# Hybrid block on one core: six tiles of the second attention allocated first, and the state-space constants recorded inside the first attention's weight units

## The chip, the cores and the metric

The kernel runs on one core of a Trainium2 chip. The metric is the device time of one execution in microseconds, as the median of several runs. The profile is of one execution.

## What is computed

The reference is one encoder block on 1024 tokens of width 1024. RMS norm; then two branches: a state-space branch and a forgetting attention of 8 heads of 128, merged by sigmoid gates; then a second norm and a retrieval of 16 of 16,384 experts for each of 8 heads (PEER). The part that the change touches:

```
step = exp(log_step)[:, None]
mag = exp(ar * step)
lam_re = mag * cos(ai * step);  lam_im = mag * sin(ai * step)
...
br = coef_re[..., None] * b_re - coef_im[..., None] * b_im
bi = coef_re[..., None] * b_im + coef_im[..., None] * b_re
...                                    # scan with lam over the tokens
s = einsum('bhqd,bhkd->bhqk', q_blk, k) * scale + c_blk[..., None] - cum
p = softmax(where(key_pos <= q_pos, s, -inf));  o = p @ v
```

## The kernel before

The tokens are worked in two groups of 512. `front(g)` is a generator for one group, and the main order (L1218 to L1240) resumes the two generators in turn. For group 0 it runs: the norm with its transposes to `hT`, a stop; the forget logits (the pool `fg`: `lg`, `cum`, `rows`), the first projections (the pool `upr`: two units of part "first", their results `ut` stored to `d_u`), then the attention (pool `att0`), the state-space scan, the gated merge, and the query of the expert search. For group 1 the scan stands before the attention `att1`. After both, `dense()` does the expert matmuls (L1135, L1195), the longest part of the time.

A weight matrix comes in units. `unit()` (L431) loads two halves of one (`wraw`, L446, on SP's queue), ScalarE makes the rounded half of `ws` (L447), VectorE (DVE) the remainder (L448), and for group 0 SP stores the split weights (`d_w`, L450) for group 1 to read back. `ws` has four buffers, so two units are in flight, and `wraw` two. An attention pass goes over four head pairs `hp`; each has the units query, key, value and gate. TensorE (PE) multiplies them at L460 (by token) and, for the gate, at L466. Then for each of the two heads: transposes of queries and keys (L640), scores (L682, L684, L686), softmax on DVE and ScalarE (L689 maximum, L692 exponential, L694, L695), transposes of the probabilities (L707, copied out at L711 and L712), product with the values (L715, L717).

`s5_setup()` (L184) is a second generator that makes the state-space constants. Up to its first `yield` it issues seven loads (L188), then one long chain of DVE instructions, most of 128x16 elements, and near the end six of 128x2304 (L340 to L345) and six of 128x2048 that leave `win` (L358 to L363). After that it stops after every small piece: eight of transposes of `win` on PE (L369, copied by ScalarE at L372, stored to `d_sw`), eight of matmuls `kz` (L387). `unit()` of part "att" in group 0 resumes it SETUP = 2 times before its own loads, and the remainder is drained at the last head pair.

What sets the order: the program is recorded as Python runs, and a scheduler then puts each engine's instructions in one fixed row, by a time line it keeps and by the order of recording. On the chip each engine takes its row in order. SP issues most DMAs and waits in its row for what they need. Tiles of a pool get addresses in the order in which they are first asked for; a tile on memory that an earlier one held waits for that one's last use. `att1` lies on the memory of the query phase of group 0: `h2T` at the bottom, above it `tops` (lists of the top search) and `sk`, `q`, `sc`, `wf`.

The main order before, of which the change drops the second resumption:

```
    first, second = front(0), front(1)
    setup = s5_setup()
    next(first)
    next(setup)
    next(first)
    next(second)
```

Of the kernel before, what the change touches and what calls it, by code (L numbers as in the profile page):

```python
# [20 lines left out]
FT = mybir.dt.float32  # L21
FR = mybir.dt.float32r
# [10 lines left out]
P = 128  # L33
# [24 lines left out]
def kernel(ctx: ExitStack, tc: tile.TileContext, x, w_in, w_f, w_query, w_out, w_glu,  # L58
# [351 lines left out]
    def pump(n, m=0):  # L410

        for i, (work, k) in enumerate(((pending, n), (gating, m))):
            left[i] += k
            while left[i] >= 1 and work:
                left[i] -= 1
                if next(work[0], True):
                    work.pop(0)
            if not work:
                left[i] = 0.0


    def front(g):
        t0, GT = GROUPS[g]
        NB, NC, B0 = GT // P, GT // L, t0 // P
# [68 lines left out]
        with tc.tile_pool(name=f"fg{g}", bufs=1, side="left", reuse_waits="tile") as sp:  # L493
# [6 lines left out]
            n = 0  # L500
# [107 lines left out]
        ap_ctx = ExitStack()  # L608
        sp = ap_ctx.enter_context(tc.tile_pool(name=f"att{g}", bufs=1, side="left", reuse_waits="tile"))
        pj = apart[0] if g else sp  # L610
        for hp in range(4):
            if g == 0 and hp == SCAN:
                for _ in setup:
# [45 lines left out]
            for h in range(2):  # L659
# [5 lines left out]
                nc.gpsimd.dma_start(rq, d_cq[hd, :, t0:t0 + GT])  # L665
                keys = [(kT[:, h], t0)]
                if g:
                    kp = sp.tile([P, 2, t0], FR, name="kp")
                    nc.gpsimd.dma_start(kp, d_k[hd][:, :, :t0])
                    vp = sp.tile([P, B0, 2, P], FR, name="vp")  # L670
                    nc.gpsimd.dma_start(vp, d_v[hd][:, :B0])
                    keys.insert(0, (kp, 0))
                probs = []
                for b in range(NB):
                    ps = psum.tile([P, S], FT, name="S", bufs=2)
                    qs = slice(b * P, (b + 1) * P)
                    for kt, k0 in keys:
                        last = k0 == t0
                        n = (b + 1) * P if last else t0
                        o = ps[:, k0:k0 + n]  # L680
                        for z, (i, j) in enumerate(PASSES):
                            nc.tensor.matmul(o, qT[:, h, i, qs], kt[:, j, :n], start=(z == 0), stop=False)  # L682
                        if last:
                            nc.tensor.matmul(o[:, n - P:n], idb, later, start=False, stop=False,  # L684
                                             skip_group_check=True)
                        nc.tensor.matmul(o, rq[:, qs], rk[:, k0:k0 + n], start=False, stop=True)  # L686
                    n = t0 + (b + 1) * P
                    nm = sp.tile([P, 1], FT, name="nm", bufs=4)
                    nc.vector.tensor_reduce(nm, ps[:, :n], axis=AX, op=OP.max, negate=True)  # L689
                    pr = sp.tile([P, n], FT, name=f"pr{b}")  # L690
                    sm = sp.tile([P, 1], FT, name="sm", bufs=4)
                    nc.scalar.activation(pr, ps[:, :n], AF.Exp, bias=nm, accum_out=sm)  # L692
                    ri = sp.tile([P, 1], FT, name="ri", bufs=4)
                    nc.vector.reciprocal(ri, sm)  # L694
                    nc.vector.tensor_scalar(pr, pr, ri, 2.0, op0=OP.mult, op1=OP.mult)  # L695
                    probs.append(pr)
                    pump(*BESIDE["score"])
# [27 lines left out]
        sp = ap_ctx.enter_context(tc.tile_pool(name=f"ssm{g}", bufs=1, side="left", reuse_waits="tile"))  # L725
# [84 lines left out]
        with tc.tile_pool(name=f"mix{g}", bufs=1, side="left", reuse_waits="tile") as sp:  # L810
# [35 lines left out]
            sp = nx.enter_context(tc.tile_pool(name=f"query{g}", bufs=1, side="left", reuse_waits="tile"))  # L846
# [369 lines left out]
    wp_ctx = ExitStack()  # L1216
    wp = wp_ctx.enter_context(tc.tile_pool(name="wraw", bufs=1, side="right"))
    first, second = front(0), front(1)  # L1218
    setup = s5_setup()
    next(first)  # L1220
    next(setup)
    next(first)
    next(second)
    next(second)
# [80 lines left out]
```

## Time and profile before

| | |
|---|---|
| median of 3 runs | 3405.45 us (3402.02 to 3405.73) |
| the profiled execution | 3406.96 us, span 3405.2 us |
| mean granted TensorE clock | 0.967 of full |
| PE busy | 3223.5 us, 95% of the span |
| DVE busy | 2596.6 us, 76% |
| ScalarE busy | 1222.5 us, 36% |
| GpSimd (POOL) busy | 1030.5 us, 30% |
| chain that ended last | PE 79%, DVE 8%, DMA 7% |

Busy time of an engine is the time in which it had an instruction in work. "PE idle" is the time between two of its matmuls. In a row of a timeline, the bracket at the end gives the idle time of the engine just before the row, and after the arrow the instruction whose end let it go on.

### The profile page before, as it was taken

To read this page: it belongs to the slowest core of one execution; us is meant where nothing else is said; L and a number is where in the kernel's file an instruction comes from. 1 tells how busy PE (TensorE), PEld (TensorE's weight loads), DVE (VectorE), ACT (ScalarE), POOL (GpSimd) and SP (SyncE) were. 2 spreads that over 40 slices of the span, in tenths; PEclk is the share of its full clock that TensorE was granted. 3 is DMA by queue.
4 is the path that set the end of the run, shared out by engine and by line. 5 is a ranking of instruction groups with operands and counts; after the bars stand their busy time and mean duration, and the time that the engine had idled before them with its cause. 6 is when DMAs were issued, how large, how long until landed. Compare 5 with 4: busy or idle time off the path is not lost.

```text
span 3405.2 us, 52100 instructions
## 1 busy us (share of the span) xinstructions
PE 3223.5 (95%) x18959; PEld 2870.8 (84%) x18959; DVE 2596.6 (76%) x5493; ACT 1222.5 (36%) x2693; POOL 1030.5 (30%) x831
## 2 busy tenths in 40 slices
PE   7899888979999797899999999999999999999998
PEld 6788677868788686789999998989889898888887
DVE  7645554688776677669898788889897888888886
ACT  4444232323455355414774222222222222222221
POOL 0000000002222021200213464555465555554553
PEclk9899798989999898899999999999999999999999
DMA  7877786757576599965979798989899899988996
GB/s 255 286 269 276 251 322 249 264 202 258 177 229 220 175 315 305 326 228 172 255 217 320 273 363 287 353 306 351 301 360 339 315 339 333 346 314 299 347 332 212
DMA packets 465315, 965.44 MB, mean 284 GB/s; under 512 B 198304, under 2 KB 226208, under 8 KB 440480
## 3 DMA queue, kind: packets, MB, share of 16 engines
q1 hardware_dynamic: 345872, 545.43, 46.9%
q0 software_dynamic: 119184, 416.67, 34.4%
q8 instruction: 149, 2.44, 0.3%
q14 instruction: 110, 0.90, 0.1%
HBM read 775.84 MB, written 186.12 MB: 283 GB/s over the span
## 4 chain that ended last, share of the span: by engine, by line
PE 79%; DVE 8%; DMA 7%; issue 3%; ACT 2%; SPq 1%; POOL 1%; DVEq 0%; ACTq 0%; POOLq 0%
PE mm L1135 25%; PE S L1195 18%; PE mm L460 10%; PE mm L466 8%; PE tp L1195 5%; PE tp L1083 4%; PE S L715 2%; PE S L682 2%; PE S L466 2%; DMA vraw<-in_uv_dram 1%; PE S L686 1%; DMA wraw<-in_w_in_dram 1%; PE tp L707 1%; DVE r L990 1%; DMA r<-in_uv_dram,idx 1%
## 5 line engine op out<-in xcount | busy, mean ns | idle before, releaser
L1135 PE MATMUL mm<-dhT,us 128*128 128x320 f32 x6144 | 973.9, 310 | 3.0 <-ACT us L1127 1.6
L1135 PEld LDWEIGHTS mm<-dhT,us 128*128 128x128 f32 x6144 | 929.1, 188 | 29.3 <-ACT us L1127 2.2
L1195 PE MATMUL S<-vs,w 128*128 128x512 f32 x3072 | 794.9, 393 | 3.6 <-ACT vs L1192 3.3
L982 POOL DMA_INDIRECT r<-in_uv_dram,idx x384 | 476.0, 1240 | 833.3 <-DVE dots L990 494.3
L982 POOL DMA_INDIRECT r<-in_uv_dram,second x384 | 518.8, 1351 | 584.4 <-DVE acc L988 419.6
L1195 PEld LDWEIGHTS S<-vs,w 128*128 128x128 f32 x3072 | 566.9, 189 | 111.1 <-ACT vs L1192 4.8
L460 PE MATMUL mm<-ws,hT 128*128 128x256 f32 x3456 | 457.1, 290 | 49.3 <-ACT qkraw L625 26.2
L988 DVE SCALAR_TENSOR_TENSOR acc<-r,dots,acc 128x1024 f32<-128x1024 f32 x384 | 491.2, 1279 | 11.0 <-DMA r<-in_uv_dram,second 8.9
L460 PEld LDWEIGHTS mm<-ws,hT 128*128 128x128 f32 x3456 | 435.5, 196 | 61.2 <-ACT qkraw L625 29.2
L990 DVE CUSTOM_DVE_ANT_0 r<-r,h 128x1024 f32<-128x1024 f32 x384 | 465.4, 1219 | 27.7 <-DMA r<-in_uv_dram,idx 27.6
L1192 ACT ACTIVATE vs<-vraw 128x512 fp32r<-128x512 f32 x256 | 160.2, 628 | 385.4 <-DMA vraw<-in_uv_dram 213.4
L1195 PE MATMUL tp<-vs,w 128*128 128x512 f32 x768 | 259.2, 392 | 2.9 <-ACT vs L1192 2.9
L1127 ACT ACTIVATE us<-uraw 128x512 fp32r<-128x512 f32 x256 | 160.1, 627 | 258.2 <-PE mm L1135 236.3
L1128 DVE TENSOR_TENSOR us<-uraw,us 128x512 fp32r<-128x512 f32 x256 | 175.0, 685 | 97.2 <-ACT us L1127 94.8
L1137 ACT ACTIVATE ag<-mm 128x320 f32<-128x320 f32 x256 | 111.3, 435 | 361.1 <-PE mm L1135 333.5
L1193 DVE TENSOR_TENSOR vs<-vraw,vs 128x512 fp32r<-128x512 f32 x256 | 174.6, 686 | 73.4 <-ACT vs L1192 71.5
L663 POOL DMA_DIRECT2D rk<-d_ck x16 | 9.3, 580 | 722.6 <-DVE t L586 372.6
L1069 ACT ACTIVATE two<-two,eT 128x128 f32<-128x128 f32 x640 | 202.5, 391 | 55.2 <-DVE two L1066 48.9
L466 PE MATMUL mm<-h2T,ws 128*128 128x512 f32 x768 | 185.0, 398 | 0.0
L1083 PE MATMUL tp<-one,two 128*128 128x128 f32 x1280 | 175.6, 284 | 8.2 <-ACT sg L1084 3.9
L1083 PEld LDWEIGHTS tp<-one,two 128*128 128x128 f32 x1280 | 165.7, 196 | 15.7 <-ACT two L1069 5.2
L1195 PEld LDWEIGHTS tp<-vs,w 128*128 128x128 f32 x768 | 143.9, 188 | 33.4 <-ACT vs L1192 3.4
(310 smaller groups left out, 3758.0 us busy)
## 6 DMA issues: line engine op xcount, KB each, us to landing
d_w<-ws SPq DMA_DIRECT2D x76, 1024.0 KB
ws<-d_w SPq DMA_DIRECT2D x76, 1024.0 KB
uraw<-in_ut_dram SPq DMA_DIRECT2D x256, 256.0 KB
vraw<-in_uv_dram SPq DMA_DIRECT2D x256, 256.0 KB
gs<-d_g SPq DMA_DIRECT2D x32, 1280.0 KB
d_g<-sg SPq DMA_DIRECT2D x40, 960.0 KB
wraw<-in_w_in_dram SPq DMA_DIRECT2D x44, 512.0 KB
d_a<-ag SPq DMA_DIRECT2D x32, 320.0 KB
```

Of the source, the lines that this page charges most:

```text
L460: nc.tensor.matmul(o, act[:, k, i, b * P:(b + 1) * P], w[k // 4][:, k % 4, j, :], start=(n == 0), stop=(n == 23))
L466: nc.tensor.matmul(o, w[k // 4][:, k % 4, i, c * P:(c + 1) * P], act[:, k, j, :], start=(n == 0), stop=(n == 3 * kk - 1))
L982: nc.gpsimd.indirect_dma_start(out=r, out_offset=None, in_=halves, in_offset=bass.IndirectOffsetOnAxis(ap=at, axis=0))
L988: nc.vector.scalar_tensor_tensor(acc, r, dots[:, k:k + 1], acc, op0=OP.mult, op1=OP.add)
L990: nc.vector.tensor_tensor_reduce(r, r, h2, 1.0, 0.0, op0=OP.mult, op1=OP.add, accum_out=dots[:, k:k + 1])
L1069: nc.scalar.activation(two[:, t, :], two[:, t, :], AF.Copy, scale=eT[:, 2, t1 + t:t1 + t + 1])
L1083: nc.tensor.matmul(pg[:, t, :], two[:, t, :], one[:, t, :], start=True, stop=True)
L1128: nc.vector.tensor_sub(us[:, :, 1, :], raw, us[:, :, 0, :])
L1135: nc.tensor.matmul(pa, parts[k // 4][:, k % 4, i, :], hT[:, k, j, ts], start=(n == 0), stop=(n == 23))
L1192: nc.scalar.activation(vs[:, 0, :], raw, AF.Copy)
L1193: nc.vector.tensor_sub(vs[:, 1, :], raw, vs[:, 0, :])
L1195: nc.tensor.matmul(out_of[b], w[:, p, b * P:(b + 1) * P], vs[:, q, :], start=(i == 0 and p == q), stop=(i == C8 - 1 and q == 1))
```

## The change

It does two things. In the second attention (g = 1) the six tiles `pr0` to `pr3`, `kp` and `vp` are allocated at the start of the pool; where they were allocated before, they are now taken from a dictionary. They get the bottom of the pool, on `h2T`; the tiles that lay there (`qT`, `kT`, `vs`, then `rk`, `rq`) move up, onto `tops`, `sk`, `q`, `sc` and `wf`. And the main order no longer resumes `setup` between the norm and the forget logits, so that the first resumption is that of the first "att" unit of group 0, the query unit of the first head pair. All instructions are the same in number on each engine.

```
         pj = apart[0] if g else sp
+        sooner = {}
+        if g:
+            sooner.update({f"pr{b}": sp.tile([P, t0 + (b + 1) * P], FT, name=f"pr{b}") for b in range(NB)})
+            sooner["kp"] = sp.tile([P, 2, t0], FR, name="kp")
+            sooner["vp"] = sp.tile([P, B0, 2, P], FR, name="vp")
+
+        def of_pool(name, shape, dtype):
+            return sooner.pop(name) if name in sooner else sp.tile(shape, dtype, name=name)
...
-                    kp = sp.tile([P, 2, t0], FR, name="kp")
+                    kp = of_pool("kp", [P, 2, t0], FR)
...
-                    vp = sp.tile([P, B0, 2, P], FR, name="vp")
+                    vp = of_pool("vp", [P, B0, 2, P], FR)
...
-                    pr = sp.tile([P, n], FT, name=f"pr{b}")
+                    pr = of_pool(f"pr{b}", [P, n], FT)
...
     next(first)
-    next(setup)
     next(first)
```

The order on DVE at the start, before: the end of the norm of group 0 (`hT`), split weights `ws`, then the state-space constants from `er` on (`lp` and `kz` are their tiles too).

```order
L448 TENSOR_TENSOR ws<-wraw,ws 128x4x256
L174 TENSOR_TENSOR hT<-tp,hT 128x4x128 x3
L275 MEMSET lp 128x16
L276 MEMSET lp 128x16
L390 MEMSET kz 128x4x128 x2
L448 TENSOR_TENSOR ws<-wraw,ws 128x4x256
L174 TENSOR_TENSOR hT<-tp,hT 128x4x128
L206 TENSOR_SCALAR er<-ls 128x16
L206 TENSOR_SCALAR en<-er 128x16
```

And with the change; `rows` is the end of the forget logits, and the four `ws` in one row are the query's and the key's weights of the first head pair, the two behind them the value's.

```order
L520 TENSOR_SCALAR rows<-rows 8x512
L521 TENSOR_SCALAR rows<-rows 8x512
L448 TENSOR_TENSOR ws<-wraw,ws 128x4x256 x4
L275 MEMSET lp 128x16
L276 MEMSET lp 128x16
L390 MEMSET kz 128x4x128 x2
L448 TENSOR_TENSOR ws<-wraw,ws 128x4x256
L206 TENSOR_SCALAR er<-ls 128x16
L206 TENSOR_SCALAR en<-er 128x16
L204 TENSOR_SCALAR en<-en 128x16
L448 TENSOR_TENSOR ws<-wraw,ws 128x4x256
```

The constants moved from behind the norm to behind the forget logits and the weights of the query, the key and half of the value. The seven loads L188 moved alike on SP's row: from before the store of the second unit's last split weights to behind the store of the key unit's.

The order on PE in the first head pair, before: the last scores of the first head, then the first `kz` matmuls, and matmuls of the next unit (L460) around the transposes of the probabilities (L707; the four tiles of probabilities have numbers).

```order
L682 MATMUL S<-kT,qT 128x512 x3
L684 LDWEIGHTS idb
L684 MATMUL S<-later,idb 128x128
L686 MATMUL S<-rk,rq 128x512
L387 MATMUL mm<-co,win 128x128 x8
L460 MATMUL mm<-ws,hT 128x256 x24
L707 MATMUL tp<-idf,pr_1401 128x128
L707 MATMUL tp<-idf,pr_1415 128x128
L707 MATMUL tp<-idf,pr_1429 128x128
L707 MATMUL tp<-idf,pr_1443 128x128
L460 MATMUL mm<-ws,hT 128x256 x23
L715 MATMUL S<-pT,vs 128x512 x2
```

And with the change, whose lines are eleven higher here (L693 is L682 of before, L718 is L707, L726 is L715).

```order
L693 MATMUL S<-kT,qT 128x512 x3
L695 LDWEIGHTS idb
L695 MATMUL S<-later,idb 128x128
L697 MATMUL S<-rk,rq 128x512
L369 MATMUL tp<-idf,win 128x128 x4
L718 MATMUL tp<-idf,pr_1393 128x128
L718 MATMUL tp<-idf,pr_1407 128x128
L718 MATMUL tp<-idf,pr_1421 128x128
L718 MATMUL tp<-idf,pr_1407 128x128
L718 MATMUL tp<-idf,pr_1421 128x128
L718 MATMUL tp<-idf,pr_1435 128x128 x2
L726 MATMUL S<-pT,vs 128x512 x2
```

The `kz` matmuls and the next unit's matmuls moved behind both heads of the first pair, where 96 of L460 stand in one row. Up to the first L369 both orders have the same matmuls.

## Rows read from the trace of the kernel before

**Rows 1.** The page's busy time, share of the span and instructions of each engine.

```profile
PE 3223.5 (95%) x18959; PEld 2870.8 (84%) x18959; DVE 2596.6 (76%) x5493; ACT 1222.5 (36%) x2693; POOL 1030.5 (30%) x831
```

**Rows 2.** Stretches: length; busy of PE, PEld, DVE, ACT, POOL; clock, DMA share, GB/s.

```profile
28.00:109.60 81.60, 77.59 (x556) 71.20 (x555) 70.48 (x234) 29.44 (x70) 1.25 (x2) 0.97 0.82 275
...
114.30:185.60 71.30, 65.73 (x441) 58.11 (x442) 33.10 (x67) 33.55 (x92) 2.59 (x4) 0.88 0.72 266
...
1160.00:1440.00 280.00, 232.04 (x1422) 209.05 (x1421) 208.16 (x385) 139.54 (x359) 60.79 (x53) 0.88 0.98 313
```

**Rows 3.** PE's timeline: start, duration, line, operation, count, idle before and releaser.

```profile
93.78 3.53 PE L460 MATMUL mm<-ws,hT 128*128 128x256 f32 x25
...
114.24 0.88 PE L369 MATMUL tp<-idf,win 128*128 128x128 f32 x6 [4.28 <-DVE win L363]
...
119.61 1.12 PE L640 MATMUL tp<-idf,qkraw 128*128 128x128 f32 x4 [2.16 <-ACT wt L372]
...
137.74 3.15 PE L460 MATMUL mm<-ws,hT 128*128 128x256 f32 x24 [0.69 <-ACT kz L391]
...
183.07 2.65 PE L460 MATMUL mm<-ws,hT 128*128 128x256 f32 x20 [0.40 <-DVE vs L653]
185.56 1.04 PE L640 MATMUL tp<-idf,qkraw 128*128 128x128 f32 x8
```

**Rows 4.** DVE's timeline in the same columns, from the constants' first row to their last.

```profile
32.92 0.18 DVE L206 TENSOR_SCALAR er<-ls 128x16 f32<-128x16 f32 x1 [1.09 <-DMA ls<-in_log_step_dram]
...
52.65 0.17 DVE L282 TENSOR_TENSOR t<-lp 128x16 f32<-128x16 f32 x1
...
76.18 1.23 DVE L448 TENSOR_TENSOR ws<-wraw,ws 128x1024 fp32r<-128x1024 f32 x1 [2.75 <-ACT ws L447]
...
111.90 2.29 DVE L363 TENSOR_TENSOR win<-win,tc 128x2048 f32<-128x2048 f32 x1
```

**Rows 5.** ScalarE's timeline at the end of the first pair's query unit.

```profile
73.94 0.38 ACT L625 ACTIVATE qkraw<-mm 128x256 f32<-128x256 f32 x1 [1.63 <-PE mm L460]
...
75.10 1.05 ACT L447 ACTIVATE ws<-wraw 128x1024 fp32r<-128x1024 f32 x1
```

**Rows 6.** SP's timeline of DMA issues: the log steps, and the key unit's second store.

```profile
29.41 0.43 SPq L188 DMA_DIRECT2D ls<-in_log_step_dram  x1
...
65.67 0.63 SPq L450 DMA_DIRECT2D d_w<-ws  x1
```

**Rows 7.** Groups by line, DVE, 52.6 to 114.25: count, busy, mean ns, idle before.

```profile
L448 DVE TENSOR_TENSOR ws<-wraw,ws 128x1024 fp32r<-128x1024 f32 x7 | 8.5, 1221 | 5.0 <-ACT ws L447 5.0
L635 DVE TENSOR_TENSOR qkraw<-qkraw,rs 128x1024 f32<-128x1024 f32 x2 | 2.4, 1220 | 0.0
L653 DVE TENSOR_TENSOR vs<-mm,vs 128x256 fp32r<-128x256 f32 x4 | 1.7, 421 | 0.2
```

**Rows 8.** DVE's timeline in the first head: maximum, last probabilities, copy of the transposed.

```profile
135.12 0.67 DVE L689 TENSOR_REDUCE nm<-S 128x1 f32<-128x512 f32 x1
...
136.84 0.49 DVE L695 TENSOR_SCALAR pr<-pr,ri 128x512 f32<-128x512 f32 x1
...
141.99 0.69 DVE L712 TENSOR_TENSOR pT<-tp,pT 128x512 fp32r<-128x512 f32 x1 [4.67 <-ACT pT L711]
```

**Rows 9.** PE's waits, 1140 to 1440: line, what for, us in total, times, longest.

```profile
PE mm L466 <- ACT tg L792: 6.9, 3, 5.1
...
PE mm L460 <- DVE tg L803: 3.6, 1, 3.6
```

**Rows 10.** PE's timeline at the start of the second attention.

```profile
755.14 31.28 PE L460 MATMUL mm<-ws,hT 128*128 128x256 f32 x240 [23.80 <-ACT qkraw L625]
...
797.39 1.07 PE L682 MATMUL S<-kp,qT 128*128 128x512 f32 x4
```

**Rows 11.** POOL's timeline at the same place.

```profile
746.31 0.75 POOL L669 DMA_DIRECT2D kp<-d_k  x1 [21.02 <-DVE tops L161]
...
785.75 1.88 POOL L982 DMA_INDIRECT r<-in_uv_dram,idx  x1 [35.37 <-DMA top<-d_s]
```

## Prediction

> **What bounds the kernel now.** I read the page's busy shares first, then a table of busy times by stretch, then TensorE's own timeline in the stretch the change touches, and last the other engines' rows that TensorE waits for there. TensorE (PE) is busy 95% of the span [rows 1], so a delay that makes PE idle is not made up later unless some later idle time of PE shrinks for a reason of its own. The stretch table [rows 2] shows where there is such idle time: 81.6 - 77.6 = 4.0 us in the first projections (28 to 109.6), 71.3 - 65.7 = 5.6 us at 114.3 to 185.6, and 280 - 232 = 48 us at 1160 to 1440.
>
> The wait that matters is the 4.28 us before 114.24 [rows 3]: PE has done the first head pair's gate matmuls and stands at the transposes of `win` (L369), the last of the state-space constants, which VectorE (DVE) writes at L363. So the constants are already the last thing to arrive there: they begin on DVE at 32.92, end at 111.90 + 2.29 = 114.2 [rows 4], and PE is only 4.3 us ahead of them. There is no slack under which a later start of this chain could hide.
>
> **The change, part by part.** (1) *The constants.* Dropping the second statement of the main order takes the seven loads and the whole chain up to `win` out of the time before the forget logits and puts them into the first "att" unit. The generator stops for the first time only behind L363, so all 194 DVE instructions still come in one piece. Nothing is added or removed; what changes is each engine's row order. On DVE the chain's first row (L206) now stands behind nine rows of the first projections and behind the split of the value unit's first weights (L448). That split ran at 76.18 in the trace, after 2.75 us of waiting for ScalarE's half of it [rows 4], which started at 75.10 [rows 5]. In the changed order ScalarE's half waits only for the end of the query unit's matmuls, which the timeline puts a little earlier (ScalarE drew the last of them at 73.94), so I take 74 to 76 us for the chain's start instead of 32.9. The loads stand on SP's queue behind the second store of the key unit's split weights, which was issued at 65.67; seven issues of 0.43 us and some 3.5 us to land (the log steps went out at 29.41 and were used at 32.92 [rows 4, 6]) end by about 73, so they are not what is late.
>
> How far does DVE get? In the old order the first part of the chain runs from 32.92 to 52.65 [rows 4], 19.7 us with the forget logits and two weight splits among it. In the new order three splits (1.22 us each), the normalisation of queries and keys and two value splits (0.42 each) stand among it instead [rows 7], about as much, so I take 20 us again, and DVE reaches the split of the next pair's first weights at about 96. That row waits for a weight buffer which the value unit's matmuls release; their last row ends at 93.78 + 3.53 = 97.3 [rows 3], plus 1.05 us of ScalarE [rows 5]: about 98.5. From there the rest of the chain remains. It took 114.2 - 52.6 = 61.6 us, in which the rows of others took 8.5 (L448 x7), 2.4 (L635 x2), 1.7 (L653 x4) and some 1.9 (eleven small normalisation rows), and the wait before the splits 5.0 [rows 7]: 61.6 - 14.5 - 5.0 = 42 us of its own, a small wait or two in it. With four weight splits and a value row between (4 x 1.22 + 0.42 = 5.3) that is 46 to 48 us: `win` is ready at 98.5 + 48 = 146.5, rounded to 147 (between 143, if the first part is quick and the small gaps close, and 151, if weight loads that now go before the stores are late). Against 114.2 this is **+33 us** (29 to 37). PE reaches the wait at 109.6 as before or two or three microseconds sooner, and idles about 37 us instead of 4.3. What PE saved by then is worth nothing, since `win` sets the end of the wait.
>
> Why can't PE do something else? PE takes its rows in order, and both orders have the same rows up to L369 (480 of L460 with the logits among them, 48 of L466). Everything of the first pair's heads stands behind it.
>
> (2) *The first two heads.* Behind `win` there is the same PE work up to the L640 at 185.56: some 430 instructions, 65.7 us busy in 71.3 [rows 2, 3]. But its order differs. Before, next unit's matmuls (L460 x24 at 137.74 and others) run while the softmax of a head is made; now both heads stand there alone and the L460 come behind them. A head's own chain is then open: from the last scores to the last probabilities 135.12 to 137.33 = 2.2 us, the copies of their transposes 0.69 on DVE [rows 8] and about as much on ScalarE ahead of it, with the hand-overs about 4 us a head, 8 in all; before, PE lost 2.2 us there in five waits, of which 0.69 at 137.74 is the longest and 0.40 at 183.07 the last [rows 3]. The first L640 moves ahead of four transposes and saves up to the 2.16 us wait at 119.61 [rows 3]. Net 8 - 2.2 - 2 = **+4 us** (0 to +10).
>
> The clock there: PE's granted clock is 0.88 of full in 114.3 to 185.6, against 0.97 before it [rows 2]; four transposes of L640 took 1.12 us at 119.61, eight took 1.04 at 185.56 [rows 3], so PE starts this stretch at its lower level (1.2 GHz) after its idle time. I have counted the start at the rows' own slow pace. By the Trainium skill (TensorE: Matmul & The Clock Gate, Part 1: The HAM clock gate) the lower level is the default and activity releases it; by that, sparse heads after 37 idle us would stay at 1.2 GHz longer than the trace shows, which is the first rival below.
>
> (3) *Later.* From about 240 us on PE's rows stand in the same order, and so does nearly everything up to the gated merge of group 0. A store and two chunk loads (`uc`) now stand behind a store of the second pair on SP: 0 to +5 us, I take 0. In 1160 to 1440 the scheduler has interleaved the merge's loads and fill matmuls differently. PE's own waits for the merge's tiles there are 6.9 us (L466 on ScalarE's tg) and 3.6 us (L460 on DVE's tg) [rows 9], beside others; I take 0, with -10 to +10. From the dense experts on the orders are alike.
>
> (4) *The second attention's pool.* `pr0` to `pr3`, `kp` and `vp` move to the bottom, onto group 0's query input, and `qT`, `kT`, `vs`, `rk`, `rq` move up onto the lists of the top search. In the trace `kp` waits 21.02 us for the lists and is issued at 746.31 [rows 11], yet its first matmul is at 797.39 [rows 10]; that is 51 us of cover. PE's 23.80 us wait that ends at 755.14 is for ScalarE's `qkraw` [rows 10], whose tile lies in another pool. Pool engine's next row, a gather, waits for the top lists themselves until 785.75 whenever `kp` goes [rows 11]. Of the tiles moved up, `qT` and `kT` are written just ahead of those scores and `vs` one unit earlier, so the lists, done by 746, have been stored long before. So **0** (-2 to +2: a slip of the first `rk`, which the scores at 800 need, or a few DVE rows put otherwise).
>
> **Sum.** 33 + 4 + 0 + 0 + 0 = +37 us. The profiled execution took 3406.96 (span 3405.2), 1.5 above the median 3405.45; 3406.96 + 37 = 3444, less 1.5: **3443 us** as a median.
>
> **Rivals.** *Clock and open heads cost more.* If PE stays at 1.2 GHz through both heads, their some 20 us of high-pace work (ten a head, by what the second head took before) grows by 8 to 15 us where it is not hidden by waits. For it: rows of 114 to 134 are at that level after only 4.28 us idle. Against: 24 matmuls of L460 took 3.15 us at 137.74, 20 took 2.65 at 183.07 [rows 3], so PE was at the higher level (2.4 GHz) again by the first. 3443 + 12 = 3455.
>
> *The merge gives it back.* One mechanism on the other side: in 1160 to 1440 PE idles 48 us [rows 2], since gate matmuls and the next norm wait for merge tiles; the new order holds blocks of up to 18 gate matmuls between expert transposes, which could fill those holes. At 12 us regained the time is 3431; it must regain over 30 us (within 0.2%, 3412) or 44 us (faster, under 3399) to decide, more than four fifths of all idle time there. Against: the waits named sum to about 20 us and the same loads still have to land on a DMA that is busy 0.98 of that stretch [rows 2].
>
> *The change doesn't delay the chain.* If DVE reached the chain early enough to have `win` by 109.6, the time would be 3405 - 4 = 3401. It would have to start about as early as before; DVE's rows in order exclude this unless the value unit's weights came 40 us sooner.
>
> **How the numbers follow.** Forecast (+22 to +48, centre 3443) 0.75; clock and open heads (3453 to 3462) 0.10; merge gives back 8 to 20 us (3423 to 3435) 0.06; merge gives back most, or the chain isn't late: 0.04 within and 0.05 under. 0.2% (6.8 us) is about what a measurement of this kernel can tell from no change: within is 3398.6 to 3412.3. So faster 0.05, same 0.04, slower 0.91. The range 3424 to 3460 leaves out the last two cases, the best of the third and the ends of the second.
>
> **What would show it.** In the profile after: L206's first row at 74 to 76; L363 ending near 147; one PE wait on DVE `win` of 35 to 39 us in place of 4.28; no L460 between the L682 of the first two heads; the L640 of 185.56 near 222; the second attention's 23.8 us wait as it is. A `win` wait under 20 us would prove the DVE count wrong; a full wait with a smaller total would put the gain in 1160 to 1440.

## The result, and the profile after

The changed kernel takes **3436.89 us** (median; 3430.64 to 3443.29), the kernel before 3405.59 beside it (3398.73 to 3408.57): a ratio of 1.0096, 95% interval 1.008 to 1.0112, that is 27 to 38 us more (the two medians alone differ by 31.3). Forecast were 3443 us, in a range of 3424 to 3460.

The profiled execution after has a span of 3428.9 us and is the shortest that was timed; against the 3405.2 of before the spans differ by 23.7 only. The page's busy line answers to [rows 1]; columns as there.

```profile
PE 3218.2 (94%) x18959; PEld 2867.4 (84%) x18959; DVE 2597.7 (76%) x5493; ACT 1226.5 (36%) x2693; POOL 1034.3 (30%) x831
```

The number of instructions is the same on each engine, so nothing was added. PE is idle for 3428.9 - 3218.2 = 210.7 us, against 3405.2 - 3223.5 = 181.7: **29 us more idle time**, and 5.3 us less busy time. Most of the latter lies in the last 48 us of both traces, in which the same kind of row was slower in the profiled execution of before, at a granted clock of 0.90 against 0.98; I put it down to that execution and not to the change. Groups by line, PE, of these 48 us (instructions, busy time and mean ns of one), of before and then of after:

```profile
L1195 PE MATMUL S<-vs,w 128*128 128x512 f32 x124 | 33.4, 412 | 0.0
```

```profile
L1206 PE MATMUL S<-vs,w 128*128 128x512 f32 x136 | 34.1, 389 | 0.0
```

With both groups of that line there PE got through 156 rows before and 172 after.

Where the idle time lies is seen in PE's timeline after (columns as in [rows 3], to which these rows answer).

```profile
94.37 11.07 PE L466 MATMUL mm<-hT,ws 128*128 128x512 f32 x48
...
139.11 0.69 PE L369 MATMUL tp<-idf,win 128*128 128x128 f32 x2 [33.68 <-DVE win L360]
...
143.77 2.70 PE L369 MATMUL tp<-idf,win 128*128 128x128 f32 x10 [3.97 <-DVE win L363]
...
148.10 1.12 PE L651 MATMUL tp<-idf,qkraw 128*128 128x128 f32 x4 [0.78 <-ACT wt L372]
...
180.85 11.75 PE L460 MATMUL mm<-ws,hT 128*128 128x256 f32 x96
...
217.32 1.03 PE L651 MATMUL tp<-idf,qkraw 128*128 128x128 f32 x8
...
792.82 1.44 PE L460 MATMUL mm<-ws,hT 128*128 128x256 f32 x5 [23.32 <-ACT qkraw L636]
```

PE is through with the first pair's gate matmuls at 105.4 and then stands for 33.68 + 3.97 = 37.65 us at the transposes of `win`, where it stood for 4.28 before; `win` has two halves, from L360 and L363, and each is waited for. The whole delay is in one place. The next table compares the times at which the two traces reach the same matmul (L651 after is L640 of before):

```
place                                      before    after     after - before
last half of win arrives (L369)            114.24    143.77    +29.5
next pair's first transposes (L640 x8)     185.56    217.32    +31.8
second attention's start (L460)            755.14    792.82    +37.7
PE's matmul no. 5000, in that attention    902.9     935.2     +32.3
behind group 0's merge                                         +28
in the dense experts                                           +29
the end                                    3405.2    3428.9    +23.7
```

Of the last 5 us regained some 4 are those of the clock at the end (16 rows more in the same time). From the wait on the difference stays between 27 and 40 us up to that place; it is largest, 40, at PE's matmul no. 2500, 475 us into the trace after.

On DVE (columns as in [rows 4], to which the first two and the last answer) the chain starts and ends so:

```profile
73.28 0.17 DVE L206 TENSOR_SCALAR er<-ls 128x16 f32<-128x16 f32 x1
...
95.18 1.23 DVE L448 TENSOR_TENSOR ws<-wraw,ws 128x1024 fp32r<-128x1024 f32 x1 [0.78 <-ACT ws L447]
...
136.77 2.29 DVE L360 TENSOR_TENSOR win<-win,tc 128x2048 f32<-128x2048 f32 x1
...
141.42 2.29 DVE L363 TENSOR_TENSOR win<-win,tc 128x2048 f32<-128x2048 f32 x1
```

L206 has no wait noted: its input was there. SP's row for the log steps, which answers to [rows 6], says the same, issued 4.2 us before DVE took them up:

```profile
69.06 0.43 SPq L188 DMA_DIRECT2D ls<-in_log_step_dram  x1
```

### The profile page after: what moved, and what is told of

Read it like the earlier page. It is cut to its first block, busy times and chain, and to the rows that moved or that the text cites. A ratio compares the mean times of both kernels' runs of the same rounds, so it can differ in the third digit from the quotient of the medians.

```text
span 3428.9 us, 52119 instructions
## 1 busy us (share of the span) xinstructions
PE 3218.2 (94%) x18959; PEld 2867.4 (84%) x18959; DVE 2597.7 (76%) x5493; ACT 1226.5 (36%) x2693; POOL 1034.3 (30%) x831
## 4 chain that ended last, share of the span: by engine, by line
PE 76%; DVE 9%; DMA 8%; issue 3%; ACT 2%; POOL 1%; SPq 0%; DVEq 0%; ACTq 0%; POOLq 0%
PE mm L1146 22%; PE S L1206 17%; PE mm L460 11%; PE mm L466 8%; PE tp L1206 4%; PE tp L1094 3%; PE S L726 2%; DMA vraw<-in_uv_dram 2%; PE S L693 2%; PE S L466 1%; DMA r<-in_uv_dram,second 1%; PE S L697 1%; POOL r L993 1%; DMA wraw<-in_w_in_dram 1%; DVE r L1001 1%
## 5 line engine op out<-in xcount | busy, mean ns | idle before, releaser
L460 PE MATMUL mm<-ws,hT 128*128 128x256 f32 x3456 | 453.4, 290 | 37.3 <-ACT qkraw L636 25.0
L460 PEld LDWEIGHTS mm<-ws,hT 128*128 128x128 f32 x3456 | 434.2, 196 | 47.4 <-ACT qkraw L636 27.1
L1094 PE MATMUL tp<-one,two 128*128 128x128 f32 x1280 | 175.2, 283 | 10.5 <-ACT sg L1095 8.4
L1094 PEld LDWEIGHTS tp<-one,two 128*128 128x128 f32 x1280 | 165.9, 196 | 17.9 <-ACT sg L1095 9.4
```

The costliest lines, as they stand in the source:

```text
L460: nc.tensor.matmul(o, act[:, k, i, b * P:(b + 1) * P], w[k // 4][:, k % 4, j, :], start=(n == 0), stop=(n == 23))
L1094: nc.tensor.matmul(pg[:, t, :], two[:, t, :], one[:, t, :], start=True, stop=True)
```

## The experiments

Two theories of the whole stood against each other. The first is that of the forecast: the constants alone cost the time, by the row order of one engine, and the second attention's pool does next to nothing. The second: what costs is something else that moved with them, such as the low clock and the unfilled heads behind the wait, or the place of the loads. Line numbers in rows are each kernel's own. Each kernel was timed with the kernel before beside it, whose median lay between 3404.9 and 3409.3 us, so kernels are compared by their ratios to it and not by their times.

### The two parts apart

In the first kernel only the constants move (the kernel before without one statement); in the second only the pool changes (the changed kernel with that statement put back).

```diff
     next(first)
-    next(setup)
     next(first)
```

> Only the second part of the change: the early resumption of the constants' generator is dropped, the pool is as before. Theory A (all of the loss is TensorE waiting for `win`, the pool costs and brings nothing): about 3437 us, 31 above the kernel before, with a wait for `win` of 37 to 38 us as in the changed kernel. Rival B (the 5.7 us that the changed kernel makes up between its first and second head pair of the second attention come from the pool's order): about 3442, and that stretch shows no gain against the kernel before.

```diff
     next(first)
+    next(setup)
     next(first)
```

> Only the first part: the six tiles at the bottom of the second attention's pool, the constants as before. Theory A: 3405.5, within 3 us of the kernel before, the 23.8 us wait at the start of the second attention unchanged. Rival B: about 3400, the gain standing in the first head pair of the second attention.

The constants alone: 3442.39 us, 1.0105 [1.0089, 1.012] of before. The pool alone: 3407.38 us, 0.9999 [0.999, 1.0008]. The first carries all of the loss: its interval overlaps that of the changed kernel. Its time is the one that rival B had named, but the second kernel, which B put at about 3400, isn't faster; what the pool does is taken up below. The first kernel's waits of PE from 90 to 160 (columns: line, what for, us in total, times, longest) are those of the changed kernel:

```profile
PE tp L369 <- DVE win L360: 33.6, 1, 33.6
PE tp L369 <- DVE win L363: 4.0, 1, 4.0
```

The pool's tile `kp` behaves as the prediction had it [rows 11]: with the pool alone it is issued at 751.37, and in the changed kernel (second row) 6.4 us ahead of PE's start at 792.82. Before, it went at 746.31, 8.8 us ahead of 755.14, so it isn't sooner by that measure. POOL's timeline, of the pool alone and of the changed kernel:

```profile
751.37 0.75 POOL L680 DMA_DIRECT2D kp<-d_k  x1
```

```profile
786.41 0.75 POOL L680 DMA_DIRECT2D kp<-d_k  x1
```

It no longer waits for `tops`, the lists, but that wait was covered anyway. What did slip, as the prediction had allowed, is the first `rk`: it was issued at 724.13 before, 31 us ahead of PE's start, and at 785.33 after, 7.5 us ahead; no wait of PE for it shows behind 792.82. A smaller effect of the pool there is taken up below.

### Is it the length of the chain before `win`?

If PE's wait is the sum of DVE rows in order, rows taken out of the chain must come back one for one. The first kernel makes `win` ahead of `cor` and `coi`, whose long rows PE doesn't wait for there. In the second the constants are incomplete: five of the seven long rows of `cor` and `coi` are left out, and nothing is moved.

```diff
-            cor = sp.tile([P, G2, 9, CH], FT, name="cor")
-            coi = sp.tile([P, G2, 9, CH], FT, name="coi")
...
             nc.vector.tensor_add(w1, w1, t8)
+            cor = sp.tile([P, G2, 9, CH], FT, name="cor")
+            coi = sp.tile([P, G2, 9, CH], FT, name="coi")
...
```

> The changed kernel, with `win` and its two inputs computed before `cor` and `coi`; the work is the same, but some five long rows (four of 2.55 us and one of 1.35) now stand behind `win` on VectorE. Theory A (TensorE waits for the length of VectorE's chain): `win` is ready about 11.5 us sooner, the wait falls from 37.6 to about 26, the time to about 3426. Rival C (the loss is in the heads that stand alone and the low clock behind the wait): the wait falls but the time stays at 3433 to 3437.

```diff
             nc.vector.tensor_mul(cor, over(Cr, 9), lam(0, 0, 9))
-            nc.vector.tensor_mul(tc9, over(Ci, 9), lam(1, 0, 9))
-            nc.vector.tensor_sub(cor, cor, tc9)
             nc.vector.tensor_mul(coi, over(Cr, 9), lam(1, 0, 9))
-            nc.vector.tensor_mul(tc9, over(Ci, 9), lam(0, 0, 9))
-            nc.vector.tensor_add(coi, coi, tc9)
-            nc.vector.tensor_scalar(coi, coi, -1.0, None, op0=OP.mult)
```

> The changed kernel without five of the seven long rows of `cor` and `coi` (four of 2.55 us, one of 1.35), so that these two constants lack their second products and the state-space branch is computed from incomplete ones. The chain is 11.5 us shorter, as in e3, but here nothing is moved behind `win`. Theory A (the wait is what the change costs): wait about 26 us, and the time follows, 3423 to 3428. Rival G (e3 gained only 4 us of its 10 because TensorE behind the shorter wait ran at the lower clock, whatever VectorE does): 3431 to 3436.

`win` first: 3433.15 us, 1.0077 [1.0063, 1.0091]. Five rows left out: 3431.19 us, 1.0079 [1.0065, 1.0093]. Both times lie in the ranges of the rivals, C and G, and not in those of theory A: the totals fall by some 6 us against the changed kernel, with intervals that overlap its own. PE's timeline shows `win` sooner in both, by 143.77 - 133.57 = 10.2 us in the first and 9.7 in the second:

```profile
133.57 2.70 PE L369 MATMUL tp<-idf,win 128*128 128x128 f32 x10 [3.96 <-DVE win L351]
```

```profile
134.11 2.71 PE L364 MATMUL tp<-idf,win 128*128 128x128 f32 x10 [3.96 <-DVE win L358]
```

So the wait follows the length of the chain. But how much of it is left when PE reaches the first `kz` matmuls, behind both heads? In the changed kernel that is at 179.94; with `win` first it is at 179.98, so in this trace all was lost again; with the rows left out it is at 173.30, and two thirds are kept there. The totals don't tell the two kernels apart, so this is a reading of one execution of each. Stretches from `win` to that place (columns as in [rows 2]), of the changed kernel, of `win` first, and of the rows left out:

```profile
143.77:179.94 36.17, 29.79 (x133) 21.70 (x133) 16.48 (x39) 15.91 (x37) 2.08 (x4) 0.77 0.24 88
```

```profile
133.57:179.98 46.41, 36.96 (x132) 26.13 (x132) 27.32 (x44) 15.80 (x37) 2.05 (x4) 0.61 0.54 171
```

```profile
134.10:173.30 39.20, 29.61 (x132) 21.49 (x132) 16.57 (x39) 15.81 (x37) 2.11 (x4) 0.75 0.25 90
```

With `win` first, DVE is busy 10.8 us longer in the stretch, since the long rows now stand ahead of the heads' own. PE idles 46.41 - 36.96 = 9.5 us there against 6.4, and is busy 37.0 us with the work that takes it 29.8 otherwise, at a clock of 0.61 against 0.77. Such a row is

```profile
143.06 2.55 DVE L359 TENSOR_TENSOR coi<-coi,tc 128x2304 f32<-128x2304 f32 x1
```

With the rows left out busy time and clock are as in the changed kernel, so an earlier start alone doesn't make the heads slow. That the long rows between the heads' own also brought the lower clock, which is the larger part of the loss, isn't shown: PE's own order differs a little too with `win` first, and the next section has the heads at 0.72 and 0.68 without such rows. The third that is lost there shows on ScalarE: the copy L367 waits 4.79 us for a store to finish (`wt` out to `d_sw`), where it waits 1.51 in the changed kernel; PE then waits 4.05 at the next transposes, against 0.78.

```profile
141.08 0.60 ACT L367 ACTIVATE wt<-tp 128x512 f32<-128x512 f32 x1 [4.79 <-DMA d_sw<-wt]
```

### Is it the clock behind the wait?

To the changed kernel 80 transposes of `bbr` are added whose result nothing reads; they depend on `bbr` alone, and so PE is at work while DVE ends the chain.

```diff
+            warm = tp_bank([P, 2, 2, P])
+            for n in range(80):
+                nc.tensor.transpose(warm[:, n % 2, n // 2 % 2, :],
+                                    bbr.rearrange("p g c -> p (g c)")[:, :P], idf)
             win = sp.tile([P, 2, G2, 8, CH], FT, name="win")
```

> The changed kernel with 80 extra transposes on TensorE whose results nothing reads; they need `bbr`, so they run in the last third of the wait for `win` and stand directly ahead of its transposes. Theory E (the first two heads, which stand alone behind the wait, take long because the granted clock there is 0.77): the clock from `win` to the first `kz` matmul rises above 0.9, that stretch falls from 36.2 us to 29 to 32, the time by 4 to 7 us to 3430 to 3433. Rival F (the hand-overs to VectorE and ScalarE set the pace of the heads): the stretch stays within 2 us of 36.

3445.49 us, 1.0114 [1.0094, 1.0134]; the interval overlaps that of the changed kernel. PE's timeline, and stretches of the transposes, of the first 8 us behind them, and from `win` to the first `kz` matmuls:

```profile
130.62 11.19 PE L355 MATMUL tp<-idf,bbr 128*128 128x128 f32 x80 [23.89 <-DVE bbr L324]
...
145.00 2.35 PE L372 MATMUL tp<-idf,win 128*128 128x128 f32 x10 [2.80 <-DVE win L366]
```

```profile
130.60:145.00 14.40, 11.58 (x83) 11.20 (x83) 14.24 (x8) 0.00 (x0) 0.00 (x0) 0.84 0.58 173
145.00:153.00 8.00, 6.66 (x28) 4.97 (x28) 2.25 (x3) 3.91 (x7) 0.00 (x0) 0.53 0.26 98
145.00:183.50 38.50, 32.46 (x132) 23.77 (x132) 16.62 (x39) 16.00 (x37) 2.11 (x4) 0.68 0.22 83
```

The clock was up during the transposes (0.84) and down again behind the pause of 2.80 us before `win` (0.53). The experiment thus didn't give the heads a high clock, and doesn't decide what one would be worth. What bounds it are traces in which the same rows ran at other clocks. In the changed kernel the first 8 us behind `win` ran at 0.50, the next 9 at 0.92, and the heads took 2.2 us more than before in all. With the constants alone (third row below), whose rows on PE are the same in the same order, they ran at 0.72 instead of 0.77 and took 38.42 us instead of 36.17.

```profile
143.77:152.00 8.23, 6.96 (x28) 5.36 (x28) 2.16 (x3) 3.81 (x7) 0.00 (x0) 0.50 0.27 98
152.00:161.00 9.00, 7.55 (x42) 5.54 (x42) 4.62 (x14) 5.25 (x13) 1.03 (x2) 0.92 0.63 235
```

```profile
145.07:183.49 38.42, 32.03 (x132) 23.25 (x132) 16.61 (x39) 16.04 (x37) 2.09 (x4) 0.72 0.23 83
```

### Does it matter which PE rows stand behind the chain?

If PE's order is at fault, the same late chain must be harmless once the transposes of `win` are put behind the first heads. In the changed kernel and then in the kernel before, the pieces of the constants are drawn only from the second head pair on.

```diff
-                for _ in range(SETUP):
+                pulls.append(0)
+                for _ in range(1 if len(pulls) == 1 else 0 if len(pulls) <= 4 else 3):
                     next(setup, None)
```

> The changed kernel, in which the first attention unit still starts the constants but the pieces that use `win` on TensorE are pulled only from the second head pair on, three for each unit. VectorE's chain starts as late as in the changed kernel. Theory A (a late chain costs only because the transposes stand on TensorE's row ahead of the first heads): the wait for `win` is gone or under 5 us, the heads have matmuls between them, the time is 3397 to 3405. Rival D (VectorE is the bound: the chain delays softmax and weight splits wherever it stands): other waits of TensorE on VectorE take its place, 3415 to 3430.

```diff
-                for _ in range(SETUP):
+                pulls.append(0)
+                for _ in range(0 if len(pulls) == 1 else 0 if len(pulls) <= 4 else 3):
                     next(setup, None)
```

> The kernel before (constants started behind the norm), with the pieces that use `win` pulled only from the second head pair on, three for each unit. Theory A with E (TensorE waits only where its row reaches `win` too soon; VectorE's chain is done by 114 as before): the 4.28 us wait is gone and the first heads have matmuls between them and full clock, 3397 to 3403. Rival D (the bound is VectorE or the pieces collide with later work): 3405 or more.

The first takes 3424.04 us, 1.0045 [1.0031, 1.0058], the second 3417.66, 1.0036 [1.0024, 1.0048]; both lie in the ranges of rival D. In the first the wait for `win` falls to 4.5 us, and by the count of PE's matmuls (their order differs here) it is at no. 700 19 us ahead even of the kernel before; 300 matmuls later it is 11 us behind, and at no. 1900 it is 22. From no. 500 to no. 1900 PE idles 31.3 us against 15.4 before, 18.6 of them between no. 700 and no. 1000, and is busy 193.4 against 185.7, at a granted clock of 0.72 from 150 to 200. The waits of PE from 100 to 200:

```profile
PE S L727 <- DVE pT L724: 5.4, 3, 3.8
PE tp L369 <- DVE win L363: 4.5, 1, 4.5
PE tp L719 <- DVE pr L707: 3.1, 1, 3.1
```

Now PE waits for softmax rows (`pT`, `pr`), since those stand between the chain's rows on DVE, and the chain ends at 168 only. Putting PE's order right takes away the 33 us wait and gives a part of it back at the heads. In the second kernel PE waits later for the weights (ScalarE's `ws`, 4.9 us) and again for `wt`; that three pieces a unit are too many is likely, but no run varies that number alone.

### The waits of the kernel before, and a version that beats both

Three kernels ask what the 4.28 us wait of the kernel before costs it [rows 3]. The first takes `win` ahead of `cor` and `coi` in it; the second draws the pieces from the value unit on (none in the query and key units), so that the transposes stand later on PE; the third does both, from the gate unit on.

```diff
-            cor = sp.tile([P, G2, 9, CH], FT, name="cor")
-            coi = sp.tile([P, G2, 9, CH], FT, name="coi")
...
             nc.vector.tensor_add(w1, w1, t8)
+            cor = sp.tile([P, G2, 9, CH], FT, name="cor")
+            coi = sp.tile([P, G2, 9, CH], FT, name="coi")
...
```

> The kernel before with `win` computed ahead of `cor` and `coi`. Theory A alone (the wait is all there is): `win` comes some 11 us sooner, the 4.28 us wait is gone, 3399 to 3403. By what e3 showed (long rows behind `win` on VectorE then stand ahead of the first softmax, and the heads stand without matmuls between them): within 3 us of the kernel before or slower, 3404 to 3412.

```diff
-                for _ in range(SETUP):
+                pulls.append(0)
+                for _ in range(0 if len(pulls) <= 2 else 2):
                     next(setup, None)
```

> The kernel before, in which the pieces that use `win` are pulled from the first head pair's value unit on, two for each unit as before, and no piece at the query and key units. Theory A (TensorE's row reached `win` two units too soon): no wait for `win` over 1 us, matmuls between the first heads, and the pieces are through as early as before; 3397 to 3402. Rival D (pieces that come later collide later, as in e6): 3406 or more.

The third has the edit of the first and

```diff
-                for _ in range(SETUP):
+                pulls.append(0)
+                for _ in range(0 if len(pulls) <= 3 else 2):
                     next(setup, None)
```

> The kernel before with `win` ahead of `cor` and `coi` and the pieces pulled from the first pair's gate unit on, two for each unit. Theory A: no wait for `win`, next unit's matmuls between all heads of the first pair; 3396 to 3402. Rival D: 3406 or more.

The first: 3408.69 us, 1.0003 [0.999, 1.0015]. In its trace, of the slowest of twelve executions (3416.91), the wait for `win` falls to 1.8 us and one of 6.9 us for ScalarE's `wt` comes up instead; ScalarE itself waits there up to 4.60 us for the earlier `wt` to be stored to `d_sw`. The third: 3416.77 us, 1.0028 [1.0017, 1.004]; in its trace PE waits for softmax rows of later heads, the longest three at 288, 358 and 380 us. From PE's waits, 165 to 440, of the third:

```profile
PE tp L708 <- DVE pr L696: 13.3, 6, 5.3
```

Of the three the second alone gains: 3402.54 us, 0.9983 [0.9974, 0.9993], although PE still waits 3.5 us for `win` where under 1 was expected. It is 10.8 us ahead at matmul no. 700 and has lost it by no. 1700, most of it in one wait of 8.5 us at 283 us for ScalarE's `ws`, split weights. The next two kernels add the pool change to it, and then also spread out 32 copies, from DRAM to DRAM, that the constants issue in one run at their end: four behind each `kz` piece.

The first of them is the second kernel's edit with the change of the pool:

```diff
-                    kp = sp.tile([P, 2, t0], FR, name="kp")
+                    kp = of_pool("kp", [P, 2, t0], FR)
...
-                for _ in range(SETUP):
+                pulls.append(0)
+                for _ in range(0 if len(pulls) <= 2 else 2):
```

> e9 with the change's new order of the second attention's pool added, the candidate for the best kernel. If the pool is worth the 1 to 2 us that TensorE idles less in the second attention with it: 1 to 2 us under e9. If it is worth nothing: as e9.

```diff
             for g0 in range(0, 32, 4):
...
+                if g0:
+                    copies(g0 - 4)
                 yield
-            o = d_sm[:, :, :]
-            for j in range(32):
-                nc.sync.dma_start(
...
+            copies(28)
```

> e11, in which the 32 copies of the shifted constants (one block on SP's queue, 21.6 us of issues at 230 to 252 in e11) are issued four at a time, one piece behind the piece whose store they read. Theory H (in e9 and e11 the block holds back the weight loads behind it, and the 9 us TensorE waits for ScalarE's `ws` near 283 give back most of what the first pair gained): that wait falls under 3 us, the time falls by 5 to 9 us against e11, to 3384 to 3388 or 0.994 of the kernel before. Rival I (the copies, spread, wait in the queue for the stores they read and hold the loads back there): the wait shows up earlier, 3390 or more.

With the pool: 3392.63 us, 0.9965 [0.9955, 0.9975]. With the copies spread too: **3387.44 us**, 0.9947 [0.9933, 0.9961], faster than both kernels, by some 50 us than the changed one; its interval still touches that of the copies in one run. The unspread copies are one row on SP's timeline, and ScalarE's row behind them waits for a load:

```profile
230.16 21.61 SPq L396 DMA_DIRECT2D d_s<-d_sm  x32
```

```profile
278.30 2.24 ACT L448 ACTIVATE ws<-wraw 128x1024 fp32r<-128x1024 f32 x2 [10.89 <-DMA wraw<-in_w_in_dram]
```

Each copy holds SP's queue for 21.61 / 32 = 0.68 us, the weights' loads are issued behind them, at 263.5, and PE waits for these. PE's waits from 100 to 345, of the copies in one run and then spread:

```profile
PE mm L461 <- ACT ws L448: 9.0, 1, 9.0
PE tp L369 <- DVE win L363: 3.5, 1, 3.5
```

```profile
PE tp L369 <- DVE win L363: 3.5, 1, 3.5
PE mm L396 <- DVE win L380: 2.2, 1, 2.2
PE tp L725 <- DVE pr L713: 1.5, 2, 0.9
```

The 9.0 us wait is gone. From matmul no. 2500 on this kernel stays 19 to 25 us ahead of the kernel before.

### What the pool does in the second attention

The same stretch, from the first matmul behind the 23 us wait to PE's matmul no. 5000, in every kernel without and with the pool change (length, and PE's idle time in it, us; with the 80 transposes the same matmul is no. 5080):

```
without: before 147.8, 9.8   constants alone 147.5, 9.5   pieces from value 146.7, 10.3
         pieces from pair two 147.0, 9.8   win first 148.3, 9.7   win first, from gate 150.9, 10.1
with:    changed 142.4, 6.3   pool alone 146.9, 7.9   win first 146.1, 7.9
         transposes later 145.6, 8.0   rows left out 145.8, 7.9   pieces and pool 142.9, 6.3
         80 transposes 146.3, 8.2   copies spread 146.7, 7.9
```

With it PE idles 6.3 to 8.2 us there, without it 9.5 to 10.3; in the three pairs that differ by the pool alone (before, constants alone, pieces from value) it saves 1.9, 3.2 and 4.0. In the changed kernel two waits of before are gone (PE's waits, 755.2 to 903, of before):

```profile
PE S L682 <- ACT pr L692: 1.7, 2, 1.4
PE S L682 <- DVE kT L643: 0.6, 1, 0.6
```

The one for `kT` is in all six kernels without the change and in none with it; the one for `pr` is in five of the six, and at most 0.3 us with it. That is the pool's gain, some 2 to 4 us. It is too small to show in the total of the pool alone (0.9999). The lengths spread more than the idle times (142 to 147 us with it), as PE's busy time also differs; why, stays open, and so does why the pool is worth more beside the later pieces (from 0.9983 to 0.9965, where 1 to 2 us were expected; the intervals touch) than alone.

## Why the prediction was right, and where it was off

**What bounds the kernel** held. That the constants were already last to arrive, with 4.28 us of PE's time ahead of them, is what made the whole of their delay visible, and the change of the constants alone, at 1.0105, is the price of it.

**The chain's start**, 74 to 76 us, was 73.28, a little ahead of the range. The loads weren't late, as argued.

**The middle of the chain** was 3.3 us too late. I let DVE reach the split of the next pair's weights at 96 and wait until the value unit's matmuls released their buffer at 97.3, and ScalarE's half after it, 98.5 in all. It ran at 95.18, after 0.78 us of waiting. The term that was off is the end of the value unit: PE came to the gate matmuls at 94.37, where it came at 97.15 before. PE's idle time from 28 us up to the `win` wait was 1.5 us instead of 4.0 [rows 2], and the 264 matmuls ahead of the gate's ran at a granted clock of 1.00 instead of 0.95. How much of this the move of the chain's rows away from the weight splits on DVE brought isn't shown: with the pool alone (third row), whose constants start early, the same matmuls ran at 1.00 too and the gate's came at 95.91.

```profile
63.50:97.15 33.65, 33.50 (x264) 33.30 (x265) 26.59 (x83) 13.27 (x46) 0.00 (x0) 0.95 1.00 323
```

```profile
62.59:94.37 31.78, 31.78 (x265) 31.78 (x266) 21.45 (x123) 14.47 (x48) 0.00 (x0) 1.00 0.87 300
```

```profile
63.76:95.91 32.15, 32.03 (x264) 31.83 (x265) 26.85 (x85) 13.30 (x46) 0.00 (x0) 1.00 1.00 316
```

I had seen that PE might come "two or three microseconds" sooner, and then wrote that what PE saved by then "is worth nothing, since `win` sets the end of the wait". But `win` hung on PE by way of that buffer, in my own working: the saving came back as an earlier `win`. The constants alone show the same link: there the gate matmuls came at 95.72, 1.35 us later than in the changed kernel, and the last half of `win` was read at 145.07, 1.30 us later.

**The rest of the chain** was 143.71 - 95.18 = 48.5 us, against 46 to 48. So `win` came at 143.7 instead of 147, and the term is **+29.5** instead of +33, at the lower end of 29 to 37. PE's wait, put at 35 to 39 us, was 37.65: right, because both of its ends came sooner.

**The first two heads** cost +2.2 us instead of +4. No L460 stands between them, as said; the waits on their softmax, which I put at about 4 us a head, came to less:

```profile
PE tp L369 <- DVE win L363: 4.0, 1, 4.0
PE tp L718 <- DVE pr L706: 3.0, 4, 0.9
PE S L726 <- ACT pT L722: 1.2, 2, 0.6
```

These are PE's waits of after from 143.7 to 217.3. Without the first, which belongs to `win`, the two heads' softmax waits sum to 4.2 us, not 8. The L640 of 185.56 came at 217.3 instead of 222. The first rival, a clock that stays low through both heads, was wrong: 0.77 on the mean up to 179.94, and 0.92 from 152 to 161. The Trainium skill's rule named for it (TensorE: Matmul & The Clock Gate, Part 1: The HAM clock gate), that the lower level is the default and activity releases it, agrees with this trace: 0.50 over the first 8 us behind the wait, and released by the sparse heads.

**Later**, where I put 0, there were +6 us up to the second attention and -5 to -10 us behind it. Two of the waits that grew are named in the trace after, from 268 to 450: 6.0 us for a load of the scan (`sw`), which was 2.0 before, and 3.0 for DVE's `qkraw`, which none before answers to (236 to 410). The bound of 0 to +5 for the loads behind the store on SP had about this size, and 0 was the wrong value to take from it; that it is these loads that made the two waits longer isn't shown.

```profile
PE mm L760 <- DMA sw<-d_s: 6.0, 1, 6.0
PE tp L651 <- DVE qkraw L646: 3.0, 1, 3.0
```

**The merge** gave back about 4 us, well within the -10 to +10. The rival that it gives most of it back was wrong. PE's waits for the merge's tile `tg`, of which [rows 9] has 6.9 and 3.6 us, sum to 12.9 before (1140 to 1480) and to 6.3 after, while others grew: that of L1094 for ScalarE's `sg` from 3.9 (L1083 of before) to 8.4. PE's waits after, 1140 to 1480:

```profile
PE tp L1094 <- ACT sg L1095: 8.4, 5, 3.6
...
PE mm L466 <- DVE tg L814: 5.3, 2, 2.8
```

**The second attention's pool**: the mechanism was right for `kp` and for the 23.8 us wait, 23.32 after. The term, 0 (-2 to +2), was too narrow: the stretch shrank by 5.4 us in the changed kernel, and idle time by 3.5, as the waits for `pr` and `kT` went. The prediction named both tiles among those that move and gave their waits no price; through which tile's memory each wait went isn't shown. The pool alone shows that this is not to be seen in the total.

**The sum** of 37 us was 31 to 33 in fact: 3.5 us less from the start of the rest of the chain, 2 less from the heads, and later terms of +6, -5 and -4 us that nearly cancel, which is luck and not foresight.

## What to carry to other kernels

Ask of a chain that already ends last which engine takes its first row, and behind what: the delay of its last row (29.5 us here, of a start 40 us later) is lost in full, however little each row takes, because PE's in-order rows cannot pass the one that waits. When PE's order is put right in turn, the chain and the heads compete for DVE, and part of the loss comes back there; a gain came from moving the consumer a few units, and a further one in the traces from spreading out the DMA issues behind it. And if a chain waits for a buffer that PE releases, what PE saves ahead of it is not lost: it moves the chain's end.

## What the runs showed of the hardware that I had not expected

PE's granted clock fell to 0.53 over 8 us behind a pause of 2.80 us that followed 11 us of unbroken transposes at 0.84, and it was 0.50 over 8 us behind the 37.65 us of waiting: behind the short pause it was about as low as behind the long one. And it fell among the small matmuls of the heads without any such pause. In the changed kernel it was 1.00 from 153.5 to 163.6 and 0.50 from 163.7 to 167.0; no wait of PE in between was over 0.8 us. The same two heads, from `win` to the first `kz` matmuls, had mean clocks of 0.77, 0.75, 0.72 and 0.68 in four kernels in which no long DVE row stood among the heads' own, and 0.61 where such rows did. So the rows of other engines may move it, but they aren't all that does, and the cause stays open.

Thirty-two copies between DRAM places take SP 21.6 us to issue, 0.68 us each, where a load of the constants took it 0.43 [rows 6]; the stores and loads right behind the copies took about as long or longer, 0.6 to 1.4 us each. While the copies were issued the DMA engines were busy 0.37 of the time only (columns as in [rows 2], of the kernel with the copies in one run), and PE's work went on:

```profile
230.00:252.00 22.00, 22.00 (x157) 20.63 (x156) 10.88 (x23) 7.64 (x16) 0.00 (x0) 1.00 0.37 97
```

What stood behind them on SP then came together (1.01 from 252 to 278.3), and the weights issued at 263.5 were taken up at 278.3. So the issuing held the weight loads back first, and the transfer of what had gathered behind it held them after; spread out, with the same number of copies, the 9.0 us wait was gone.
